# Two sets of DRAM weight sums moved from behind the residual's loads into the pool stage, in a one-layer hybrid decoder kernel

## The chip, the cores and the metric

The kernel runs on one core of one Trainium2 chip. The metric is the device time of one execution in microseconds (us); of several runs the median is given. TensorE (PE in the profile) multiplies matrices, VectorE (DVE) and ScalarE (ACT) work on tiles in SBUF and PSUM, GpSimd (POOL) and SyncE (SP) are used here mostly to issue DMA transfers. Every engine works off its own queue in order.

## The reference

One decoder layer with 16 learned tokens put ahead of 512 positions of width 1024, all in float32. Cut to what matters here:

```python
u = rmsnorm(h, mix_norm_w[i])
proj = u @ w_in[i]                        # pool, z, xbc, dt and gate columns
gates = jax.nn.sigmoid(proj[..., OFF_GATE:] + b_gate[i])
y_pool = pool_mixer(u_pool, pool_w_group[i], pool_scale[i]) @ w_pool_up[i]
y_ssd = mamba2_branch(z, xbc, dt_raw, ...) @ w_ssd_out[i]
h = h + (gate_pool * y_pool + gate_ssd * y_ssd) @ w_o[i]
v = rmsnorm(h, mlp_norm_w[i])
hid = jax.nn.relu(v @ w_ff1[i])           # 1024 -> 4096
h = h + (hid * hid) @ w_ff2[i]            # 4096 -> 1024
out = rmsnorm(h, final_norm_w)            # the 16 tokens are dropped
```

`pool_mixer` takes, for four groups of 256 channels, the mean over the last 2, 4, 8 or 16 positions less the value itself, and multiplies each group by a 256x256 matrix.

## The kernel before

Every float32 product is made of three products in a rounded format: each operand is split into a high part (a cast on ScalarE, tiles `whi`, `shi`) and the residue (a subtraction on VectorE, `wlo`, `slo`), and TensorE multiplies high by high, high by low and low by high. So each weight block of 128x1024 (512 KB) that SyncE loads (`raw`) costs a cast, a subtraction and its matmuls. `raw` tiles come from a pool of three, and SyncE waits for one to be free before it issues the next load.

Large products are done by a scheme with seven instead of eight partial products (Winograd's form of Strassen's). It needs sums of weight quarters, called t1, t2, s3 and t4. These are not formed on an engine: GpSimd issues DMA transfers from DRAM to DRAM, plain copies and accumulating ones, that build the sums in DRAM tiles (`wsum`; `f_t`, `f_s` in the profile). One such group is a set. There are 15 sets, in a fixed order: two for the scan's weights (`fx`), six for `w_ff1` (`f1`), seven for `w_ff2` (`f2`). A set of `fx` or `f1` is 8 transfers of 512 KB, four of them accumulating; a set of `f2` is 4, two of them accumulating. An accumulating transfer waits on GpSimd's queue until the copy that it adds to has landed, and blocks the queue while it waits.

The stages, in order of time in the profile:

- 0 to about 470 us: norm, projections and the scan of eight groups. The first 11 sets are issued here, spread out by a list `SETS_AT` and tied to small copies on GpSimd (L800).
- about 470 to 553 us: the pool stage. GpSimd loads back the accumulator (`acc`, L1056) and the gates (`m1`, L1090; `m<-gate_d` in the profile). `pool_pair` (L976 on) is called four times: it loads two weight blocks (L126), forms sums of their halves on VectorE (`sm`, and the first block overwritten; L985 to L990), splits them (`split_form`, L132 and L133: whiA, whiS, whiD, whiB and wloA to wloB) and makes seven products on TensorE (L1004, L1007), of which VectorE makes the moving averages (`pw`, `pu`). `pool_mix` multiplies by the group matrix (`pg`), `gate_ssd` makes the second gate (`pgs`).
- about 553 to 629 us: the merge (`pup` and the remaining `pgs`).
- about 629 to 671 us: the product with `w_o` (`wo_...`), added to the residual tile `ht`, which GpSimd loads at L1202 as soon as its SBUF, held by `u` until the last gate's matmul, comes free. Behind these four loads GpSimd issues what is left of the sets.
- about 671 us to the end: the MLP. `ff1_plain` (`pf`), `ff1_pair` (`px`) and `prod` (`alpha`, `p`, `q`: the products with `w_ff2`), which `onto` (L1240) adds to `ht` on VectorE.

The program is written in one order; a planner then orders each engine's queue by that order, by what is ready, and by edges. `with tc.issue_after(x)` gives an edge to `x` to those instructions of the block that are on the same engine as `x`, and to no others. The lines that the change touches, and the transfers of a set:

```python
def weight_steps():
    t = sets.pop(0)
    ...
    yield put(o["t1"], src[B11])                          # L777
    yield put(o["s3"], src[B12])                          # L778
    yield put(o["t1"], src[B12], accum_op=ALU.add)        # L779
    if "t2" in o:
        yield put(o["t2"], src[B22])                      # L781
    yield put(o["s3"], src[B22], accum_op=ALU.add)        # L782
    if "t2" in o:
        yield put(o["t2"], o["t1"], accum_op=ALU.add)     # L784
        yield put(o["t4"], src[B21])                      # L785
        yield put(o["t4"], o["t2"], accum_op=ALU.add)     # L786
```

```python
for t in range(4):
    ht_load = nc.gpsimd.dma_start(ht[:, t, :], x[t * P : (t + 1) * P, :])   # L1202
while sets:
    with tc.issue_after(ht_load.ins):
        ht_load = weight_sums()
```

`weight_sums()` issues one whole set and returns its last transfer. `SETS_POOL` is 0 before, so that four sets are left for the loop behind the `ht` loads: f1 number 4, f2 number 5, f1 number 5, f2 number 6, in that order, 24 transfers. The sets numbered f1 4 and f2 5 are read in the last part of the MLP.

## Time and profile before

| | us |
|---|---|
| median of 3 runs (999.92 to 1001.16) | 1000.0 |
| the profiled execution's own time | 1001.71 |
| its span, first to last instruction | 1000.0 |
| TensorE busy | 987.8 |
| VectorE busy | 803.9 |
| ScalarE busy | 602.2 |
| GpSimd busy | 119.5 |

In the rows of the profile, `out<-in` names the tiles an instruction writes and reads, L is the line of the kernel, x the number of instructions, and the brackets say how long the engine stood idle before it and what ended that. In the timeline a row begins with start and duration in us. In the rows of DMA issues the last number is the median time from issue to landing. SPq and POOLq mark the queue that issued a transfer.

### The profile page before, as it was taken

The numbers are of one execution on the slowest core, as the hardware profiler recorded it, in microseconds if no ns is written. First come the engines' busy times: TensorE is split into PE (matmuls) and PEld (weight loads), VectorE is DVE, ScalarE is ACT, GpSimd is POOL, SyncE is SP. The second block draws the span as 40 slices with busy tenths as digits, with TensorE's granted clock in tenths as the row PEclk, the third lists the DMA queues.
The fourth block names the chain that finished last, engine by engine and source line by source line (L and its number), as shares of the span: only waits on it lengthen the run. The fifth ranks groups of instructions, "written<-read, shape, count | busy, mean of one in ns | idle before, by whom it ended". The sixth has DMA issues, their size and how long they took to land.

```text
span 1000.0 us, 15672 instructions
## 1 busy us (share of the span) xinstructions
PE 987.8 (99%) x6035; PEld 873.8 (87%) x6035; DVE 803.9 (80%) x1162; ACT 602.2 (60%) x855; POOL 119.5 (12%) x215
## 2 busy tenths in 40 slices
PE   9999999999999999999999999999999999999997
PEld 7889998989889999978898888888789999999986
DVE  7978997879845888988789666975988888888885
ACT  7657839495924658574345433477666656656654
POOL 0011321211212212223200001121000000000000
PEclk9999999999999999999999999999999999999999
DMA  7284968666798848768723723899354454454332
GB/s 261 78 254 149 268 197 214 190 191 212 230 271 235 245 129 259 226 163 171 271 85 127 253 85 112 228 243 314 92 190 148 148 190 144 152 186 150 129 106 85
DMA packets 61803, 184.52 MB, mean 185 GB/s; under 512 B 7072, under 2 KB 8416, under 8 KB 60704
## 3 DMA queue, kind: packets, MB, share of 16 engines
q1 hardware_dynamic: 39456, 109.00, 32.7%
q0 software_dynamic: 18240, 67.51, 26.4%
q10 hardware_dynamic: 4032, 7.00, 1.9%
q8 instruction: 47, 0.77, 0.3%
q14 instruction: 28, 0.23, 0.1%
HBM read 173.13 MB, written 58.59 MB: 232 GB/s over the span
## 4 chain that ended last, share of the span: by engine, by line
PE 93%; ACT 3%; DVE 2%; DMA 1%; issue 0%; SPq 0%; ACTq 0%; DVEq 0%
PE px L1465 8%; PE px L215 8%; PE alpha L1533 6%; PE pz L215 6%; PE px L1468 4%; PE px L218 4%; PE alpha L1536 3%; PE pgp L215 3%; PE pz L218 3%; PE pgs L215 3%; PE py L694 2%; PE pqx L509 2%; PE pso L146 1%; PE pgp L218 1%; PE wo_alpha L1226 1%; PE po L688 1%
## 5 line engine op out<-in xcount | busy, mean ns | idle before, releaser
L113 DVE TENSOR_TENSOR wlo<-raw,whi 128x1024 fp32r<-128x1024 f32 (+2 forms) x88 | 102.0, 1171 | 46.8 <-ACT whi L111 31.0
L111 ACT CAST whi<-raw 128x1024 fp32r<-128x1024 f32 (+2 forms) x88 | 87.2, 1011 | 70.3 <-PE pso L147 15.3
L215 PE MATMUL px<-uh,whi 128*128 128x264 f32 (+1 forms) x320 | 80.9, 291 | 0.0
L218 PE MATMUL px<-ul,whi 128*128 128x264 f32 (+1 forms) x320 | 78.8, 285 | 0.0
L1240 DVE TENSOR_TENSOR ht<-ht,alpha 128x1024 f32<-128x1024 f32 x35 | 42.7, 1220 | 29.1 <-PE alpha L1533 29.1
L215 PEld LDWEIGHTS px<-uh,whi 128*128 128x128 f32 x320 | 60.4, 189 | 0.9 <-issue 0.7
L1162 ACT CAST shi<-rawf 128x1024 fp32r<-128x1024 f32 x42 | 44.2, 1053 | 28.0 <-PE alpha L1536 18.3
L218 PEld LDWEIGHTS px<-ul,whi 128*128 128x128 f32 x320 | 60.2, 188 | 0.4 <-issue 0.2
L1533 PE MATMUL alpha<-shi,hh 128*128 128x512 f32 x140 | 55.3, 395 | 2.0 <-DVE ht L1240 1.9
L1536 PE MATMUL alpha<-shi,hl 128*128 128x512 f32 x140 | 54.7, 391 | 0.0
L1163 DVE TENSOR_TENSOR slo<-rawf,shi 128x1024 fp32r<-128x1024 f32 x42 | 51.2, 1219 | 0.6 <-ACT shi L1162 0.6
L1468 PE MATMUL px<-vsl,shi 128*128 128x256 f32 x192 | 47.4, 280 | 0.0
L1465 PE MATMUL px<-vsh,shi 128*128 128x256 f32 x192 | 47.4, 281 | 0.0
L215 PE MATMUL pz<-uh,whi 128*128 128x512 f32 x112 | 43.7, 390 | 0.0
L218 PE MATMUL pz<-ul,whi 128*128 128x512 f32 x112 | 43.6, 389 | 0.0
L215 PE MATMUL px<-uh,wlo 128*128 128x264 f32 (+1 forms) x320 | 41.8, 283 | 0.0
L215 PEld LDWEIGHTS px<-uh,wlo 128*128 128x128 f32 x320 | 39.9, 188 | 0.0
L1533 PE MATMUL alpha<-slo,hh 128*128 128x512 f32 x140 | 37.4, 389 | 0.0
L1465 PEld LDWEIGHTS px<-vsh,shi 128*128 128x128 f32 x192 | 36.2, 188 | 0.9
L1468 PEld LDWEIGHTS px<-vsl,shi 128*128 128x128 f32 x192 | 36.1, 188 | 0.9
L1468 PE MATMUL px<-vl,shi 128*128 128x256 f32 x144 | 36.1, 283 | 0.0
L1465 PE MATMUL px<-vh,shi 128*128 128x256 f32 x144 | 36.0, 282 | 0.0
(599 smaller groups left out, 3064.8 us busy)
## 6 DMA issues: line engine op xcount, KB each, us to landing
raw<-in_w SPq DMA_DIRECT2D x96, 512.0 KB, 4.4
f_t<-in_f POOLq DMA_DIRECT2D x38, 512.0 KB, 7.4
f_s<-in_f POOLq DMA_DIRECT2D x26, 512.0 KB, 7.3
b<-in_f SPq DMA_DIRECT2D x21, 512.0 KB, 4.5
rawf<-in_f SPq DMA_DIRECT2D x36, 256.0 KB, 2.9
rawf<-f_t SPq DMA_DIRECT2D x36, 256.0 KB, 2.9
abc<-acs_d POOLq DMA_DIRECT2D x8, 1024.0 KB, 7.6
f_t<-f_t POOLq DMA_DIRECT2D x12, 512.0 KB, 6.7
```

The lines of the kernel that those rows point to most:

```text
L111: act.copy(hi[:, c], raw[:, c])
L113: dve.tensor_tensor(lo[:, c], raw[:, c], hi[:, c].bitcast(F32), op=ALU.subtract)
L215: pe.matmul(o, wt, rhs[0][k][:, c], start=part == 0 and k == 0, stop=part == 1 and k == NK - 1)
L218: mm[0] = pe.matmul(o, wt, rhs[1][k][:, c], start=False, stop=False)
L509: at = pe.matmul(o, wk, f[k][0], start=start and not low and k == 0, stop=stop and low == 1 and k == 3, skip_group_check=True)
L1162: splits.append((act.copy(hi, src), dve.tensor_tensor(lo, src, hi.bitcast(F32), op=ALU.subtract)))
L1163: dve.tensor_tensor(lo, src, hi.bitcast(F32), op=ALU.subtract)))
L1240: added[0] = dve.tensor_tensor(o, o, src, op=op)
L1465: pe.matmul(ps, m, f[k][0], start=start and not low and k == 0, stop=stop and low == 1 and k == 3, skip_group_check=True)
L1468: pe.matmul(ps, m, f[k][1], start=False, stop=False, skip_group_check=True)
L1533: pe.matmul(ps[t], hh[:, p, seg, st], m, start=bool(first and not low and p == 0), stop=bool(last and low and p == 1), skip_group_check=True)
L1536: pe.matmul(ps[t], hl[:, p, seg, st], m, start=False, stop=False, skip_group_check=True)
```

## The change

The first two of the four remaining sets (f1 number 4 and f2 number 5, 12 transfers) are issued behind the last load of a gate in the pool stage, at the turn n = 1 of its loop, by an edge on GpSimd's queue. The unused loop at the head of the stage is taken out. The two sets that are left stay behind the `ht` loads.

```diff
-SETS_POOL = 0
+SETS_POOL = 2
...
     for d in range(NK):
         t_load = nc.gpsimd.dma_start(acc[d], acc_d[d])
-    for _ in range(SETS_POOL):
-        with tc.issue_after(t_load.ins):
-            t_load = weight_sums()
     pend = [pooled_halves(*a) for a in pool_pair(POOL_ORDER[0])]
...
             for d in MERGE:
                 with tc.issue_after(mixed[0].ins):
                     if d < NK - 1:
-                        nc.gpsimd.dma_start(m1[d], gate_d[d])
+                        t_load = nc.gpsimd.dma_start(m1[d], gate_d[d])
+            for _ in range(SETS_POOL):
+                with tc.issue_after(t_load.ins):
+                    t_load = weight_sums()
```

## The prediction

> **What bounds the kernel now.** I read the page first, then the table of stretches, then the waits of TensorE, then the order of time around its one late wait.

> ```profile
> PE 987.8 (99%) x6035; PEld 873.8 (87%) x6035; DVE 803.9 (80%) x1162; ACT 602.2 (60%) x855; POOL 119.5 (12%) x215
> ```

> TensorE (PE) is busy for 987.8 of 1000.0 us. Whatever the change does to the queues, it can only give back what TensorE idles behind the place that it touches, or open a new idle time there. So the question is where TensorE idles from 488 us on, the earliest time at which a moved transfer can start.

> ```profile
> core 0: us, PE busy (x) PEld busy (x) DVE busy (x) ACT busy (x) POOL busy (x), PEclk, DMA share, GB/s
> 488.00:525.00 37.00, 37.00 (x243) 34.12 (x242) 33.67 (x50) 15.84 (x24) 0.16 (x1) 1.00 0.33 118
> 619.00:665.00 46.00, 46.00 (x211) 37.98 (x211) 38.00 (x46) 22.91 (x37) 11.81 (x19) 1.00 0.84 240
> 665.00:692.00 27.00, 27.00 (x127) 22.30 (x127) 16.46 (x31) 20.98 (x40) 4.91 (x7) 1.00 1.01 301
> 720.00:740.00 20.00, 18.00 (x102) 15.41 (x101) 18.67 (x24) 11.52 (x16) 0.00 (x0) 1.00 0.51 160
> ```

> Each row is a stretch: TensorE's busy time comes second, the granted clock (1.00 throughout) and the share of the 16 DMA engines stand near the end. TensorE is full in the first three and lacks 2.00 us in the last. The transfers, on the other hand, are at 0.33 in the pool stage and at their limit (1.01) from 665 to 692 us. The waits of TensorE, and then its timeline and VectorE's (DVE), say what the 2 us are:

> ```profile
> PE alpha L1533 <- DVE ht L1240: 1.9, 1, 1.9
> ```

> ```profile
> 719.70 1.07 PE L1533 MATMUL alpha<-slo,hh 128*128 128x512 f32 x4
> ...
> 725.37 0.47 PE L1533 MATMUL alpha<-shi,hh 128*128 128x512 f32 x1 [1.89 <-DVE ht L1240]
> ```

> ```profile
> 724.01 1.22 DVE L1240 TENSOR_TENSOR ht<-ht,alpha 128x1024 f32<-128x1024 f32 x1
> ```

> One product of the second MLP matrix ends at 720.77 us. The next one into the same bank must wait until VectorE has added the first to `ht`. VectorE could have begun at 720.8 and begins at 724.01, because its queue is behind. Where it fell behind is seen some 35 us earlier, on ScalarE (ACT) and on VectorE:

> ```profile
> 681.03 1.18 ACT L1571 ACTIVATE ht<-ht,m 128x1024 f32<-128x1024 f32 x1
> 686.24 1.05 ACT L111 CAST whi<-raw 128x1024 fp32r<-128x1024 f32 x1 [4.04 <-DMA raw<-in_w]
> ```

> ```profile
> 687.33 1.23 DVE L113 TENSOR_TENSOR wlo<-raw,whi 128x1024 fp32r<-128x1024 f32 x1 [5.40 <-ACT whi L111]
> ```

> ScalarE is free at 682.2 and stands 4.04 us for a weight block; VectorE stands 5.40 us behind it. The DMA issues of two stretches give that block's landing time (issued at 673.15), and that of six others of the same size issued between 577 and 620 us:

> ```profile
> raw<-in_w SPq DMA_DIRECT2D x1, 512.0 KB, 13.0
> ```

> ```profile
> raw<-in_w SPq DMA_DIRECT2D x6, 512.0 KB, 3.4
> ```

> 13.0 us instead of 3.4. GpSimd's (POOL's) queue shows whose transfers are in the way:

> ```profile
> 486.41 1.75 POOL L1090 DMA_DIRECT2D m<-gate_d  x3 [0.37 <-DMA raw<-in_w]
> 619.06 1.58 POOL L1202 DMA_DIRECT2D ht<-in_x  x3 [130.90 <-PE pgs L215]
> 620.85 0.53 POOL L1202 DMA_DIRECT2D ht<-in_x  x1 [0.21 <-issue]
> 621.37 0.53 POOL L777 DMA_DIRECT2D f_t<-in_f  x1
> ...
> 656.21 0.82 POOL L782 DMA_DIRECT2D f_s<-in_f  x1 [0.43 <-DMA f_s<-in_f]
> 656.75 0.83 POOL L777 DMA_DIRECT2D f_t<-in_f  x1
> ```

> After the last gate load (488.2 us) the queue stands 130.90 us for the residual's tile, then issues four weight-sum sets one after another. The first two, twelve transfers, are all issued from 621.37 to 656.21; the third starts at 656.75 and, with the fourth, fills the stretch in which the block was late.

> **The change part by part.** It adds no transfer and no arithmetic: 12 transfers of 512 KB (8 for the set of `w_ff1`, 4 for that of `w_ff2`) move from behind the four `ht` loads to right behind the last gate load. That edge holds on GpSimd's own queue; the `with` on `mixed[0]`, a ScalarE instruction, holds nothing there, as the gate loads leave by 488 us, long before that mix. So the moved sets start at about 488.2.

> What leaves the tail: the two sets that stay now take the place of the first two. Their form is the same (8 and then 4 transfers), so by the rows above they are issued from about 621.4 to 656.2, and the last two land some 8 us later, about 664 (my estimate from the landing of the last addition, issued at 656.21). The four `ht` loads stay where they are and meet the same company. From 665 on SyncE's (SP's) loads have the DMA engines to themselves. Of the 13.0 us only the neighbours on SyncE's own queue are left; even three blocks of 3.4 us one after another would be 10.2 us, so the block would be there by 683.4, and by overlap probably by 677; ScalarE needs it at 682.2. I take the wait of 4.04 us as gone. VectorE then starts its backlog about 4 us sooner. It needs 3.25 us (724.01 less 720.77) to meet the product on time. So TensorE's 1.89 us go, and with them the remaining 0.11 of the 2.00, a gap at 730.0 behind the next addition to `ht`. The first matmul after a wait takes 0.47 us, which I count as 0.1 more. Sum here: minus 2.1 us. It can't be more, since TensorE has no other wait behind 488 us worth naming; it is nothing if VectorE is late for another reason.

> What the pool stage gets: twelve transfers beside the loads of its weights. By the old spacing from first issue to last landing (621.4 to 664, 42.7 us) they end at 531 at the latest; with fewer loads ahead of them I expect about 525. GpSimd waits between them for its own earlier transfers; queued behind are only the `ht` loads, which can't go before 619.06, so that wait has 88 us of cover. Their bytes are read back only in the second half of the MLP. What is exposed is SyncE's loads between 488 and 531. Two have little cover. The first is the second weight block of the third pair, in SyncE's queue, its landing time, and the VectorE rows that follow it:

> ```profile
> 507.19 0.33 SPq L126 DMA_DIRECT2D raw<-in_w  x1
> ```

> ```profile
> raw<-in_w SPq DMA_DIRECT2D x1, 512.0 KB, 3.4
> ```

> ```profile
> 511.76 0.69 DVE L985 TENSOR_TENSOR sm<-raw,raw 128x512 f32<-128x512 f32 x1
> ...
> 519.14 1.22 DVE L133 TENSOR_TENSOR wloD<-raw,whiD 128x1024 fp32r<-128x1024 f32 x1
> ```

> ```profile
> 520.65 0.65 PE L1004 MATMUL pxx<-t0h,wloD 128*128 128x264 f32 x4
> ```

> It lands at 510.6 and is first read at 511.76: 1.2 us free. From there VectorE runs without a pause to the residue `wloD`, ready at 520.36, and TensorE uses that at 520.65: 0.3 us free. So a load that takes longer than 4.9 us (3.4 + 1.2 + 0.3) stops TensorE by the excess. The second is the first block of the fourth pair, issued at 520.39:

> ```profile
> 524.00 1.06 ACT L132 CAST whiA<-raw 128x1024 fp32r<-128x1024 f32 x1 [3.25 <-DVE pu L1026]
> ```

> ```profile
> 528.66 0.68 DVE L974 TENSOR_TENSOR pl<-pu,ph 128x512 fp32r<-128x512 f32 x1
> ```

> ```profile
> 530.17 0.39 PE L147 MATMUL pg<-pl,whi 128*128 128x512 f32 x1
> ```

> Its cast follows 3.6 us after the issue, so at once on landing; both queues run in order, and the `pl` that TensorE reads at 530.17 is ready at 529.34. There 0.8 us are free, and a load of over 4.4 us costs the excess.

> No row shows these loads beside such sums, so I bound them by loads that were. Here are, from two earlier stretches, a load issued at 409.88 beside one accumulating transfer (issued at 409.80), and one issued at 154.04 beside an accumulation (153.99), a plain copy and a store:

> ```profile
> f_t<-in_f POOLq DMA_DIRECT2D x1, 512.0 KB, 6.2
> raw<-in_w SPq DMA_DIRECT2D x1, 512.0 KB, 3.6
> ```

> ```profile
> raw<-in_w SPq DMA_DIRECT2D x1, 512.0 KB, 9.6
> ```

> By the first both places cost nothing. By the second the first place costs 4.7 us and the second 5.2, less what the first already gave it in time. At 507 us I expect the dependent accumulation of the set alone in flight (it stood 18 us behind the start in the old order), at 520 the last two additions. That is nearest to the 3.6 us, and I take 0; a gain is excluded, as TensorE has no idle time there (37.00 of 37.00).

> [...]

> The sum: the profiled execution took 1001.71 us, its span 1000.0 and 1.7 around it; it becomes 999.6, span 997.9. The median of the runs shown is 1000.0, 1.7 below that execution, and less 2.1 it is **997.9 us**.

> **The rivals.** *The pool stage eats part of it.* One or both tight loads take 5 to 7 us: 0.3 to 2.1 us lost, time 998.2 to 1000.0. For it: landing times near the sums vary from 3.6 to 9.6. Against it: the pool stage's DMA engines are at 0.33.

> *Slower: the weight block of the third pair comes late.* If the end of the first set and the two copies that open the second coincide with the load at 507.19, as at 154.04, it takes 9.6 us, VectorE stops at `sm`, and TensorE stops at the residue for 4.7 us: 1000.0 - 2.1 + 4.7 = 1002.6; with the second place late too, up to 1005. It decides from a load of 7.0 us on (4.9 + 2.1). For it: VectorE is busy for 33.67 of 37 us there, so that nothing is caught up, and the set's transfers come in bursts. Against it: by the spacing in the old order the burst falls 6 to 8 us behind that load's issue or, if the set runs faster, just beside the landing.

> *The stall stays.* VectorE may be late for its own amount of work: it is busy for 18.67 of 20 us at the stall. Then nothing is gained: 1000.0. Against it: it had 5.40 us of idle time on one row in the same backlog.

> *The order changes.* The order on the queues is a planner's; moved transfers may let it put VectorE's or ScalarE's instructions another way. One 128x1024 subtraction (1.22 us) ahead of a residue that has 0.3 us free costs 0.9; a few would undo the gain and more: 999 to 1003. Nothing in the profile speaks for it.

> **How the numbers follow.** 0.2%, 2.0 us, is about what a measurement of this kernel can tell from no change. The forecast, 0.50, lies 2.1 us below, just over that line: 0.38 over it and 0.12 short of it. Part eaten: 0.14, within. Slower by the late block: 0.24, of which 0.22 beyond 2 us and 0.02 within. Stall stays: 0.06, within. Order: 0.06, 0.04 slower and 0.02 within. Together faster 0.38, same 0.36, slower 0.26. The range begins at 997.2, since the runs shown spread by 1.2 us and the gain has a ceiling; above it takes in the first late load at its bound (1002.6) and leaves out both late: 1002.8. The likeliest case alone is 997.2 to 998.6.

> **What would show it.** Right: f-set transfers on GpSimd from 488 to about 525; the block of 673 us landing in under 9; no wait of `whi` near 686 and none of `alpha` on `ht` near 725; TensorE full from 490 to 550. Wrong: a wait of TensorE on `wloD`, `whiS` or `pl` in the pool stage, with `sm` idle on a DMA before it; or the `alpha` wait still there although the block landed early; or a different order on VectorE.

## The result and the profile after

| | before | after |
|---|---|---|
| median, us (4 runs each, one chip) | 1000.58 | 1007.38 |
| lowest to highest, us | 999.92 to 1001.93 | 1005.47 to 1008.22 |
| the profiled execution, us | 1001.71 | 1007.03 |

The ratio is 1.0065 (95% interval 1.0053 to 1.0077): the change costs 6.8 us, where 997.9 us was forecast and 1002.8 was the upper end. The order of instructions on TensorE, VectorE, ScalarE and SyncE is the same in both kernels; only GpSimd's queue differs, by the twelve transfers. In the changed kernel the gate loads are L1087 instead of L1090.

The tail looks as forecast. The table of stretches of the changed kernel (columns as before):

```profile
526.00:530.00 4.00, 4.00 (x20) 3.29 (x19) 0.33 (x1) 0.58 (x1) 0.00 (x0) 1.00 0.97 324
530.00:534.00 4.00, 2.02 (x7) 0.82 (x5) 3.49 (x5) 2.38 (x5) 0.00 (x0) 1.00 0.23 95
534.00:538.00 4.00, 3.20 (x8) 2.56 (x9) 4.00 (x8) 1.50 (x2) 0.00 (x0) 0.51 0.00 0
538.00:542.00 4.00, 4.00 (x22) 3.82 (x21) 2.90 (x4) 1.47 (x4) 0.00 (x0) 0.64 0.00 0
...
665.00:692.00 27.00, 27.00 (x134) 22.43 (x133) 21.29 (x38) 23.80 (x49) 0.00 (x0) 1.00 0.60 186
720.00:740.00 20.00, 20.00 (x102) 16.95 (x101) 18.59 (x28) 12.90 (x18) 0.00 (x0) 1.00 0.46 145
```

From 665 to 692 the DMA engines are at 0.60 instead of 1.01, and from 720 to 740 TensorE lacks nothing. The loss is in the first four rows: TensorE is busy for 2.02 of 4 us from 530 on, and in the two stretches of 4 us behind that its granted clock is 0.51 and 0.64 on average. Its waits, and its own timeline there:

```profile
PE pg L147 <- DVE pl L974: 2.3, 2, 1.2
...
PE pg L146 <- ACT ph L973: 0.5, 1, 0.5
```

```profile
527.91 0.39 PE L215 MATMUL pgs<-uh,whi 128*128 128x512 f32 x1
528.14 0.39 PE L218 MATMUL pgs<-ul,whi 128*128 128x512 f32 x1
...
531.32 0.50 PE L146 MATMUL pg<-ph,whi 128*128 128x512 f32 x1 [0.52 <-ACT ph L973]
532.99 0.50 PE L147 MATMUL pg<-pl,whi 128*128 128x512 f32 x1 [1.17 <-DVE pl L974]
533.33 0.39 PE L146 MATMUL pg<-ph,whi 128*128 128x512 f32 x1
534.80 0.80 PE L147 MATMUL pg<-pl,whi 128*128 128x512 f32 x1 [1.09 <-DVE pl L974]
...
536.25 0.63 PE L146 MATMUL pg<-ph,whi 128*128 128x512 f32 x1
536.67 0.63 PE L147 MATMUL pg<-pl,whi 128*128 128x512 f32 x1
```

Three waits, 2.78 us in all. Behind the third, matmuls of the same size start 0.42 us apart (536.25 to 536.67), where it was 0.23 ahead of the first (527.91 to 528.14). What TensorE waits for is on ScalarE's and VectorE's timelines:

```profile
529.42 1.05 ACT L132 CAST whiA<-raw 128x1024 fp32r<-128x1024 f32 x1 [7.54 <-DMA raw<-in_w]
530.38 0.37 ACT L1030 COPY pu<-pxx 128x264 f32<-128x264 f32 x1
530.65 1.14 ACT L973 CAST ph<-pu 128x512 fp32r<-128x512 f32 x2
```

```profile
530.51 1.22 DVE L133 TENSOR_TENSOR wloA<-raw,whiA 128x1024 fp32r<-128x1024 f32 x1 [4.18 <-ACT whiA L132]
531.65 0.69 DVE L962 TENSOR_TENSOR pw<-pw 128x513 f32<-128x513 f32 x1
532.25 0.69 DVE L974 TENSOR_TENSOR pl<-pu,ph 128x512 fp32r<-128x512 f32 x1
...
534.06 0.68 DVE L974 TENSOR_TENSOR pl<-pu,ph 128x512 fp32r<-128x512 f32 x1
```

`ph` and `pl` need nothing of the fourth pair's block, but they stand behind its cast and its residue in two in-order queues. ScalarE stands 7.54 us for the block. This is the second place of the prediction. The landing times in the changed kernel: the load issued at 521.52 (the second place), that of 508.33 (the first place), that of 680.71 (the block of the tail), and the two additions of the second set, issued at 519.00 and 520.25:

```profile
raw<-in_w SPq DMA_DIRECT2D x1, 512.0 KB, 7.8
...
raw<-in_w SPq DMA_DIRECT2D x1, 512.0 KB, 4.3
...
raw<-in_w SPq DMA_DIRECT2D x1, 512.0 KB, 4.6
...
f_t<-in_f POOLq DMA_DIRECT2D x1, 512.0 KB, 5.3
...
f_s<-in_f POOLq DMA_DIRECT2D x1, 512.0 KB, 8.8
```

The tail's block takes 4.6 us instead of 13.0, and the first place's 4.3 is under its 4.9. The second place's load took 3.5 us before and takes 7.8 beside the two additions.

All these kernels make TensorE's matmuls in one order (but for a dozen between 543 and 563 us in the two kernels that load a block again), so the start of each can be compared with that of the same matmul in the first profile of before. The rows are the kernels of the next section. The table gives how much later a kernel is at 488 us of that profile, and by how much that lag grows in each stretch behind it. 488 us is before the change can act; what stands in the column "by 488" is the difference of two executions.

| lag, us | by 488 | 488 to 528 | 528 to 530.3 | 530.3 to 560 | 560 to 719 | 719 to 726 | end |
|---|---|---|---|---|---|---|---|
| after | +1.12 | +0.02 | +3.49 | +2.93 | 0 | -2.14 | +5.31 |
| after, again | +2.21 | -0.02 | +4.37 | +1.72 | -0.04 | -2.14 | +5.99 |
| one set moved | +0.57 | -0.02 | 0 | 0 | -0.02 | -2.13 | -1.73 |
| sets in the merge | +2.23 | -0.02 | 0 | 0 | +1.20 | -2.13 | +1.14 |
| halves first | +2.17 | +0.50 | +0.01 | +0.79 | -0.05 | -2.13 | +1.15 |
| load doubled | -0.41 | +0.16 | +4.08 | +2.69 | 0 | -0.39 | +6.17 |
| half load doubled | +0.96 | -0.02 | +3.35 | +1.45 | 0 | -1.17 | +4.61 |
| additions plain | +1.25 | +0.21 | +0.85 | +0.41 | -0.01 | -2.14 | +0.43 |
| split | +0.76 | +1.34 | 0 | 0 | 0 | -2.13 | -0.14 |
| three sets early | +0.70 | -0.03 | +0.01 | -0.01 | -0.02 | -2.13 | -1.62 |
| six copies | +1.53 | -0.02 | 0 | 0 | -0.02 | -2.13 | -0.75 |

"528 to 530.3" holds the stop and the slow restart, "530.3 to 560" the halved clock.

### The profile page after: what moved, and what is told of

It reads as the page before. It is cut to its first block, busy times and chain, and to the rows that moved or that the text cites. A ratio compares the mean times of both kernels' runs of the same rounds, so it can differ in the third digit from the quotient of the medians.

```text
span 1005.3 us, 15673 instructions
## 1 busy us (share of the span) xinstructions
PE 992.2 (99%) x6035; PEld 877.0 (87%) x6035; DVE 804.3 (80%) x1162; ACT 602.1 (60%) x855; POOL 120.6 (12%) x215
## 4 chain that ended last, share of the span: by engine, by line
PE 92%; ACT 3%; DMA 2%; DVE 2%; issue 0%; SPq 0%; ACTq 0%; DVEq 0%
PE px L1465 8%; PE px L215 8%; PE alpha L1533 6%; PE pz L215 6%; PE px L1468 4%; PE px L218 4%; PE alpha L1536 3%; PE pgp L215 3%; PE pz L218 3%; PE pgs L215 3%; DMA raw<-in_w 2%; PE py L694 2%; PE pqx L509 2%; PE po L688 2%; PE pso L146 1%; PE pgp L218 1%
## 5 line engine op out<-in xcount | busy, mean ns | idle before, releaser
L113 DVE TENSOR_TENSOR wlo<-raw,whi 128x1024 fp32r<-128x1024 f32 (+2 forms) x88 | 101.9, 1171 | 42.2 <-ACT whi L111 24.5
L111 ACT CAST whi<-raw 128x1024 fp32r<-128x1024 f32 (+2 forms) x88 | 87.2, 1010 | 67.6 <-PE pso L147 15.3
L215 PE MATMUL px<-uh,whi 128*128 128x264 f32 (+1 forms) x320 | 80.9, 291 | 0.0
L1240 DVE TENSOR_TENSOR ht<-ht,alpha 128x1024 f32<-128x1024 f32 x35 | 42.7, 1219 | 29.2 <-PE alpha L1533 29.2
L215 PEld LDWEIGHTS px<-uh,whi 128*128 128x128 f32 x320 | 60.5, 189 | 0.9 <-issue 0.7
L1533 PE MATMUL alpha<-shi,hh 128*128 128x512 f32 x140 | 55.2, 395 | 0.0
L215 PE MATMUL pz<-uh,whi 128*128 128x512 f32 x112 | 43.7, 391 | 0.0
L215 PE MATMUL px<-uh,wlo 128*128 128x264 f32 (+1 forms) x320 | 41.8, 283 | 0.0
L215 PEld LDWEIGHTS px<-uh,wlo 128*128 128x128 f32 x320 | 39.9, 189 | 0.0
L1533 PE MATMUL alpha<-slo,hh 128*128 128x512 f32 x140 | 37.4, 390 | 0.0
## 6 DMA issues: line engine op xcount, KB each, us to landing
raw<-in_w SPq DMA_DIRECT2D x96, 512.0 KB, 4.6
f_t<-in_f POOLq DMA_DIRECT2D x38, 512.0 KB, 6.8
f_s<-in_f POOLq DMA_DIRECT2D x26, 512.0 KB, 6.7
b<-in_f SPq DMA_DIRECT2D x21, 512.0 KB, 4.6
f_t<-f_t POOLq DMA_DIRECT2D x12, 512.0 KB, 6.5
```

The costliest lines, as they stand in the source:

```text
L111: act.copy(hi[:, c], raw[:, c])
L113: dve.tensor_tensor(lo[:, c], raw[:, c], hi[:, c].bitcast(F32), op=ALU.subtract)
L215: pe.matmul(o, wt, rhs[0][k][:, c], start=part == 0 and k == 0, stop=part == 1 and k == NK - 1)
L1240: added[0] = dve.tensor_tensor(o, o, src, op=op)
L1533: pe.matmul(ps[t], hh[:, p, seg, st], m, start=bool(first and not low and p == 0), stop=bool(last and low and p == 1), skip_group_check=True)
```

## The experiments

**Is it the second set's additions?** The first of the two sets alone is moved.

```diff
-SETS_POOL = 2
+SETS_POOL = 1
```

> Only the first of the two sets (f1 number 4, eight transfers) is moved into the pool stage; f2 number 5 stays behind the residual's loads, with the two others. Theory A (the loss comes from the second set's two additions, which meet the weight load of about 521 us; TensorE stops 2.8 us and its clock is then halved for 6 us): the moved set is issued by about 515 us and has landed by about 520, so that load takes 3.4 to 4.4 us as before, TensorE does not wait for pl near 531 and keeps a clock of 1.00 there. Behind the residual there are 16 transfers instead of 12, issued from 621 to about 668, so most of the 1.9 us wait at 725 is still saved: 998 to 1000.5 us. Rival B (any weight sums in the pool stage cost the time, whichever transfers they are): a wait of 1 to 3 us in the pool stage and a halved clock remain, 1002 to 1006 us.

Measured 1000.16 us beside 1000.99 of the kernel before on the same chip (0.9994, 0.9986 to 1.0003). The load at 520.94 and a stretch:

```profile
raw<-in_w SPq DMA_DIRECT2D x1, 512.0 KB, 3.6
```

```profile
530.00:534.00 4.00, 4.00 (x24) 3.49 (x24) 4.00 (x7) 3.02 (x4) 0.00 (x0) 1.00 0.00 0
```

TensorE is full, its clock 1.00. The time is within theory A's figures; rival B's wait and lower clock aren't there: the eight transfers of the first set in the pool stage cost nothing in this profile.

**Does the load cost only by the order of the queues?** All transfers stay; the casts and subtractions of the pooled halves (`halved_by` holds the second pair's last ones) go ahead of the block's.

```diff
-        fa = split_form(a1, both, f"A{p}")
-        behind = behind or (None, None)
+        with after(*(halved_by if p == POOL_ORDER[3] else ())):   # the last ph, pl
+            fa = split_form(a1, both, f"A{p}")
+        behind = behind or ((halved_by[1], None) if p == POOL_ORDER[3] else (None, None))
```

> The changed kernel with all its transfers where they are; two edges put the cast and the subtraction of the fourth pair's first block (whiA, wloA), and the sum sm, behind the casts ph and the subtractions pl of the second pair on ScalarE's and VectorE's queues. Theory A (the load is late, but it costs only because ph and pl stand behind its cast in two in-order queues): the load of 521 us still takes 6 to 9 us, but ph and pl are done by about 526 and TensorE does not wait at 531; at most 1 us is lost where wloA or wloS is first used; clock 1.00: 998 to 1000.5 us. Rival C (the transfers slow TensorE directly, or the lower clock comes from something other than its waiting): clock again near 0.5 to 0.6 for some us behind 534, 1003 to 1007 us.

Measured 1000.76 (1.0002, 0.9992 to 1.0011). The landing of the block (issued at 523.20) and ScalarE's timeline:

```profile
raw<-in_w SPq DMA_DIRECT2D x1, 512.0 KB, 7.6
```

```profile
527.49 1.14 ACT L975 CAST ph<-pu 128x512 fp32r<-128x512 f32 x2 [0.19 <-DVE pu L964]
530.83 1.05 ACT L132 CAST whiA<-raw 128x1024 fp32r<-128x1024 f32 x1 [2.20 <-DMA raw<-in_w]
```

The load is as late as in the changed kernel (7.6), yet TensorE doesn't stop near 531 and its clock stays at 1.00 there: `ph` is cast before the block lands. The median is 0.3 us above theory A's figures and far below rival C's. These edges give back nearly all of the 6.8 us of the change, with every transfer where it was. What is lost there is 0.50 and 0.79 us (table). The 0.50 is the first place: the load of 509.34 took 5.2 us, over its 4.9. The 0.79 is lost from 538 to 541, at the products that use the fourth pair's `whiD`.

**Does the wait halve the clock, or do the transfers?** No set is moved. The fourth pair's first block is loaded twice, one more 512 KB load on SyncE's queue, with edges that keep the queues near their order; in essence:

```diff
+        for _ in range(again):          # 1, for the fourth pair's first block
+            nc.sync.dma_start(a1, w[block])
```

> The kernel before, with no sets moved, and with the first weight block of the fourth pair loaded twice into the same tile (one more 512 KB load on SyncE's queue, which waits for the first to land); edges keep the order of ScalarE, VectorE and TensorE there near to that of before, ph and pl behind whiA and wloA. Theory A (a stop of TensorE of 2 to 3 us in all near 531 us halves its clock for some 6 us, whatever made it stop): the block is there 3.3 to 4 us later than before, TensorE waits 2.3 to 3 us, and its clock falls to about 0.5 for 4 to 7 us: 1004 to 1007 us. Rival C (the halved clock comes from GpSimd's transfers or from the DMA engines at their limit): only the wait, clock 1.00: 1002.5 to 1003.7 us.

Measured 1007.50 beside 1000.99 (1.0059, 1.0047 to 1.0072), 0.5 us above theory A's figures.

```profile
530.90 0.49 PE L148 MATMUL pg<-ph,whi 128*128 128x512 f32 x1 [1.50 <-ACT ph L980]
532.99 0.80 PE L148 MATMUL pg<-pl,whi 128*128 128x512 f32 x1 [1.59 <-DVE pl L982]
```

```profile
530.00:534.00 4.00, 1.51 (x3) 1.01 (x4) 4.00 (x6) 1.96 (x4) 0.00 (x0) 0.77 0.00 0
534.00:538.00 4.00, 4.00 (x11) 3.16 (x10) 3.96 (x6) 2.67 (x3) 0.00 (x0) 0.50 0.00 0
```

With no transfer of GpSimd near, and the DMA engines at 0.00 in both stretches, TensorE waits 3.09 us and its clock is 0.50 behind. Rival C falls: the clock is halved behind the stop without those transfers. The same with half of the block:

> As the kernel with the doubled load (nothing of the sets moved), but only half of the fourth pair's first block is loaded a second time, a smaller dose of the same delay. By theory A the block is complete 2 to 3 us later than before and TensorE waits 1 to 2.2 us in all near 531. Whether its clock is then halved tells where the point lies between the 1.9 us after which it stayed at 1.00 at 725 us and the 3.1 us after which it fell: if it falls, 1002.5 to 1005 us; if not, 1001.5 to 1003 us.

Measured 1005.65 (1.0051, 1.0032 to 1.0069).

```profile
531.36 0.50 PE L148 MATMUL pg<-ph,whi 128*128 128x512 f32 x1 [0.77 <-ACT ph L980]
533.45 0.79 PE L148 MATMUL pg<-pl,whi 128*128 128x512 f32 x1 [1.59 <-DVE pl L982]
```

```profile
534.00:538.00 4.00, 4.00 (x15) 3.19 (x14) 3.96 (x6) 2.89 (x4) 0.00 (x0) 0.66 0.00 0
```

It was not a much smaller dose: 2.36 us of waits where 1 to 2.2 were expected, and the clock falls here too (1.45 us lost), so that the time is 0.65 us above the figures for that.

**Is it that they accumulate?** The second set's two additions become plain copies.

```diff
-        yield put(o["t1"], src[B12], accum_op=ALU.add)
+        yield put(o["t1"], src[B12], **({} if t == ("f2", 5) else {"accum_op": ALU.add}))
```

(and the same for `s3`; the sums of this set are left out)

> The changed kernel with the second set's two additions turned into plain copies of the same pieces (the sums of that set are left out): the same number of transfers at the same places, none of them accumulating beside the load of 521 us. [...] Theory G (any two GpSimd transfers there do it): the load takes over 6.5 us, waits of 2 us or more and the halved clock stay, ratio 1.004 to 1.007.

Measured 1002.95 beside 1001.00 (1.0019, 1.0010 to 1.0028). The load at 521.97, TensorE's wait, and the stretch behind it:

```profile
raw<-in_w SPq DMA_DIRECT2D x1, 512.0 KB, 5.0
```

```profile
PE pg L147 <- DVE pl L975: 0.7, 1, 0.7
```

```profile
534.00:538.00 4.00, 4.00 (x32) 3.88 (x31) 4.00 (x7) 2.07 (x4) 0.00 (x0) 1.00 0.00 0
```

The load takes 5.0 us, one short wait of 0.7 us is left and the clock stays at 1.00: the load of over 6.5 us and the ratio of 1.004 to 1.007, which theory G had for any two transfers of GpSimd, aren't there. Of the 4.3 us that the load was late in the first profile of the changed kernel, the accumulating form made 2.8. The two copies landed sooner than the additions, too (4.1 and 5.4 us against 5.3 and 8.8). The prediction's row of 3.6 us also had an addition beside the load, but a single one, issued 0.08 us ahead of it; here there are two, issued 2.5 and 1.3 us ahead. Which of these two differences counts was not tried.

**Elsewhere.** Both sets in the merge:

```diff
+        if n == 3:                      # loop of the merge
+            t_load = pool.tensor_copy(seen, acc[d][:, :1])
+            for _ in range(SETS_POOL):
+                with tc.issue_after(t_load.ins):
+                    t_load = weight_sums()
```

> Both sets are taken out of the pool stage and issued in the merge instead, tied to a small GpSimd copy at about 575 to 581 us, so that all twelve transfers are issued before the residual's loads at 619. Theory A: the pool stage is that of the kernel before (load of 521 us in 3.5 us, no wait for pl, clock 1.00), the wait at 725 us is gone as in the changed kernel, and the merge's weight loads have cover: 998 us, 997.5 to 999. Rival B (twelve transfers between loads stop TensorE wherever they are put): a new wait of TensorE on wlo or whi between 580 and 615 us, 1000 to 1005 us.

Measured 1002.03 (1.0010, 1.0001 to 1.0018): theory A missed, and though the time is within rival B's figures, its wait between 580 and 615 us isn't there. The copy came at 596.29, not at 580, so the sets were still running when the residual's turn came. GpSimd's queue and TensorE's waits:

```profile
624.55 0.82 POOL L782 DMA_DIRECT2D f_s<-in_f  x1 [0.47 <-DMA f_s<-in_f]
625.09 2.46 POOL L1204 DMA_DIRECT2D ht<-in_x  x4
```

```profile
PE wo_q L1231 <- DVE l_m L1105: 1.1, 1, 1.1
```

The `ht` loads leave at 625.09 instead of 619.06, VectorE waits 1.16 us for them, and TensorE behind it. The two remaining trials put the second set, or the second and a third, at n = 0 of that loop, with the first in the pool stage:

> The first of the two sets (f1 number 4) in the pool stage as in the changed kernel, the second (f2 number 5, four transfers) in the merge, tied to a small GpSimd copy behind the first gated sum at about 560 us; the two last sets stay behind the residual's loads. Theory A: the four transfers run from 560 to about 577 us beside merge loads that have cover, the load of 521 us takes 3.5 us, no wait and no lower clock near 531, and the wait at 725 us is gone: 998.0 to 999.5 us on a chip where the kernel before takes 1000.6 to 1001, that is 0.9975 to 0.9990 of it. Rival D (the gain of the tail is less in most executions than the 1.9 us of the profiled one): 0.9990 to 1.0000.

> As the last, with a third set (f1 number 5, eight more transfers) put into the merge as well, from about 577 to 605 us, so that only f2 number 6 is left behind the residual's loads. Theory A: the tail from 640 to 692 us is now almost free of weight sums, no new wait elsewhere: like the split kernel or up to 0.5 us better, 0.9970 to 0.9990 of the kernel before. Rival B (weight sums stop TensorE wherever weight loads have to be shared): a wait of 1 us or more between 580 and 640 us, 1.0000 or above.

Measured 1001.04 (1.0001, 0.9989 to 1.0014) and 1000.57 (1.0000, 0.9987 to 1.0014), beside 1000.78. No stop and no lower clock near 531, the wait at 725 gone, no new wait between 580 and 640, and still no gain: this speaks for rival D. In the first of them the load of the first place (507.93) took this:

```profile
raw<-in_w SPq DMA_DIRECT2D x1, 512.0 KB, 6.0
```

and the lag grew by 1.34 us from 488 to 528. The pool stage is the same as with one set moved and with three sets early, where this load took 4.2 and 4.7 us and the lag grew by nothing: whether the first place is late differs from execution to execution.

**Where is the gain?** The changed kernel and the kernel before once more, for further profiles.

> The changed kernel once more, for the spread of its executions beside those of the kernel before on the same chip. Theory A: again waits for ph and pl near 531 us of 2 to 3.5 us in all and a halved clock behind them of 4 to 7 us; 1.005 to 1.008 of the kernel before. Rival E (the waits and the lower clock of the first profile were an accident of one execution): the waits are under 1 us in this profile, ratio under 1.003.

> The kernel before once more, for a second profile. Theory A: the wait for ht at 725 us is 1.9 us again, so that the tail's gain is worth as much in most executions. Rival D (that wait varies): it is under 1.2 us here.

The changed kernel again: 1007.50 beside 1000.78 (1.0059, 1.0038 to 1.0079), with the second place's load at 8.7 us. So that is no accident of one execution. But the wait of the kernel before at 725 us is. Its second profile has no row for `alpha` at all among the waits. Four more profiles of it followed.

> The kernel before, a third profile, to see in how many of its executions TensorE waits near 725 us. Theory H (the block issued at about 673 lands at a time that the queue of sums sets, about 686; TensorE reaches 725 earlier or later by what it has lost before, so that the wait is 1.9 us where it has lost least and nothing where it comes 1.5 us later): if TensorE starts the matmuls of 719.70 in the first profile within 0.3 us of that time, the wait is 1.5 to 2.1 us; if it starts them over 1 us later, the wait is under 0.7 us.

> The kernel before, a fourth profile, with the same expectation as the third: the sum of what TensorE lost ahead of 719 us (against the first profile) and its wait near 725 us is 1.5 to 2.3 us by theory H; by rival D, that the wait comes and goes with the DMA engines alone, the two are unrelated.

> The kernel before, a fifth profile, for the count of executions with the wait near 725 us. Theory I: under 0.7 us. Rival: 1.5 to 2.1 us.

> The kernel before, a sixth profile, as the fifth. Theory I: under 0.7 us. Rival: 1.5 to 2.1 us.

| profile of before | 1st | 2nd | 3rd | 4th | 5th | 6th |
|---|---|---|---|---|---|---|
| lag at 719 us against the 1st | 0 | +1.54 | +1.05 | +2.61 | +0.22 | +3.18 |
| lag gained from 719 to 726 | 0 | -1.79 | -1.72 | -1.78 | -1.94 | -2.13 |
| wait for `ht` near 725 | 1.9 | none | 0.2 | none | none | none |

The wait of 1.9 us is in one of six, and one of 0.2 us in another. In the fifth, TensorE came as early as in the first, but the block (issued at 673.37) was there sooner; its landing, ScalarE's wait for it, and the stretch:

```profile
raw<-in_w SPq DMA_DIRECT2D x1, 512.0 KB, 11.1
```

```profile
684.55 1.05 ACT L111 CAST whi<-raw 128x1024 fp32r<-128x1024 f32 x1 [1.06 <-DMA raw<-in_w]
```

```profile
720.00:740.00 20.00, 19.86 (x116) 17.20 (x115) 18.09 (x22) 12.34 (x17) 0.00 (x0) 1.00 0.59 181
```

11.1 us instead of 13.0 is enough. So theory H, by which TensorE's own lateness sets the wait, doesn't hold in general. It fits the third profile; in the fourth there is no wait, as by H, but the lag of 2.61 is already above the sum of 1.5 to 2.3 that H gave; it doesn't fit the fifth. The kernel with the doubled load, whose tail is that of before, speaks against it too: TensorE comes 6.5 us later there, the same block is issued at 679.67 and takes 12.6 us, and the wait is 1.5 us. Taking the two sets from the tail gains 0 to 0.4 us there in five profiles of six (the difference of the lags from -2.13), and not 2.1. The upper bound was tried too: six plain copies in place of the two sets, whose additions are left out.

```diff
+        if t in (("f1", 4), ("f2", 5)):
+            for n, q in zip(o, (B11, B12, B22, B21)):
+                yield put(o[n], src[q])
+            return
```

> The changed kernel with the two moved sets replaced by six plain copies (the additions of these two sets are left out), issued at once from 489 us. Nothing waits for a transfer of their own, the copies have landed by about 502 us, and the tail is that of the changed kernel. So this is the most that taking the two sets from the tail can give. Theory I (the 1.9 us wait of the first profile is there in a minority of the executions of the kernel before): ratio 0.9990 to 1.0005. Rival (it is there in most, and something in the pool stage or the merge ate the gain of the other kernels): 0.9970 to 0.9985.

Measured 999.98 beside 1001.96 (0.9984, 0.9974 to 0.9994), which is outside theory I's figures and inside the rival's. What speaks for theory I is the count of the profiles, not this time. On this chip 9 of 17 runs of the kernel before had a mean granted clock of 0.998 or less, and one of the 12 of this kernel. In five of the seven profiles with such a mean and no lower clock behind 531, the clock is halved for a while near 446 us, ahead of anything that differs; in the other two it is lower only at the end of the span. Among the runs with a mean of 0.999 or more the medians are 999.74 (11 runs) and 1000.53 (8 runs), 0.8 us apart. How much of the 0.16% is the emptied tail, these runs don't settle.

## Why the prediction was wrong, point by point

- **What bounds the kernel**: right. All that moved the time is where TensorE stops, or runs at a lower clock behind a stop, and the order on its queue did not change (the rival of the planner's order falls).
- **The gain of 2.1 us**: the mechanism was read rightly and was seen to vanish (block in 4.6 us, TensorE full from 720 to 740), but its size was one execution's. The step that failed is the sum: it took a wait from an execution of 1001.71 us and subtracted it from a median of 1000.0, of executions of which, going by the six profiles, most have no such wait. The prediction named the 1.7 us between the two and did not ask whether the wait was part of it. In size: 2.1 forecast, 0 to 0.4 in five of six profiles. The kernels with fewer sets in the tail and no stop in the pool stage (one set moved, three sets early, six copies) measure 0.9994, 1.0000 and 0.9984 of the kernel before.
- **The first place**: threshold about right. By the prediction a load that takes longer than 4.9 us "stops TensorE by the excess": loads of 4.3, 5.2 and 6.0 us cost 0.02, 0.50 and 1.34, which is some 0.2 us more than the excess. Its price of 0 was right in both profiles of the changed kernel, in part by luck: with the same transfers it was 0.50 in the kernel of the halves.
- **The second place**: threshold right, value wrong, and this is the step that decided. The excess over 4.4 is 3.4 us for 7.8 and 4.3 for 8.7; the lags are 3.49 and 4.37. I put two additions beside that load and took the row of 3.6 us, a load beside one addition, as the nearest. The row of 9.6 us, with an addition and two more transfers, came nearer to what was measured. The timing was called right ("the last two additions" at 520); the price was not.
- **The slower rival**: right in kind, wrong in its place. It put the late block at the third pair; it was the fourth pair's. Even its 1005 us for both places late, which the range left out, is 2.4 us under what was measured.
- **What had no price at all**: the clock, which the sum left at 1.00 behind a stop. A stop of 2.4 to 3.7 us cost 1.4 to 2.9 us more. With this the medians close: 3.5 to 4.4 for the stop, 1.7 to 2.9 for the clock, next to nothing from the tail, 6.1 to 6.4 together, against 6.8 and 6.7 measured.

## What to carry to other kernels

Before a wait of one profile is priced as a gain, take a second profile of the unchanged kernel: the wait of 1.9 us was in one of six here. Price a moved transfer by what it runs beside and by its form (7.8 us for the load beside two additions, 5.0 beside two copies), put the excess over the cover on the bill, and add a second item for the clock: behind stops of 2.4 to 3.7 us near 531 it cost 1.4 to 2.9 us more here (the section below has the rows). Where a late load stops work that doesn't need it, try a few edges in the order of the queues: here they were worth nearly as much as moving the transfers back (1000.76 us beside 1000.99 of the kernel before).

## What was not expected of the hardware

TensorE's clock. These stops and the clock behind them were seen (us waited, lowest granted clock in stretches of 4 or 5 us):

| where | waited | clock behind |
|---|---|---|
| additions plain, 531 | 0.7 | 1.00 |
| merge, 637 | 1.1 | 1.00 |
| 441 to 444, all 17 profiles | 1.4 to 1.5 | 1.00 in 10, lower in 7 |
| load doubled, 731 | 1.5 | 1.00 |
| first profile of before, 725 | 1.9 | 1.00 |
| half load doubled, 531 | 2.36 in two | 0.66 |
| after, 531 | 2.78 in three | 0.51 |
| load doubled, 531 | 3.09 in two | 0.50 |
| after again, 531 | 3.7 in three | 0.65 |

The row of 441 to 444 as the stretch of 444 to 449 shows it, in the first profile of before and in its fourth, the same instructions behind the same wait:

```profile
444.00:449.00 5.00, 4.93 (x35) 3.92 (x36) 5.00 (x7) 2.72 (x5) 1.80 (x2) 1.00 0.72 100
```

```profile
444.00:449.00 5.00, 4.31 (x24) 3.38 (x25) 5.00 (x9) 3.01 (x5) 1.80 (x2) 0.72 0.60 66
```

Such an episode is worth some 1.6 us (the lag of the first profile of the changed kernel grows by 1.58 from 440 to 449 us), and it is a part of the spread between executions of one kernel.

```profile
530.67:534.08 3.41, 1.35 (x4) 0.48 (x3) 3.41 (x6) 1.71 (x4) 0.00 (x0) 1.00 0.08 32
534.08:537.49 3.41, 2.69 (x6) 2.18 (x7) 3.41 (x7) 0.99 (x2) 0.00 (x0) 0.50 0.00 0
537.50:540.91 3.41, 3.41 (x14) 3.10 (x13) 3.19 (x5) 1.43 (x2) 0.00 (x0) 0.50 0.00 0
540.91:544.32 3.41, 3.41 (x30) 3.41 (x29) 1.57 (x4) 1.85 (x3) 0.00 (x0) 1.00 0.00 0
...
530.60:534.01 3.41, 1.74 (x7) 0.89 (x5) 1.57 (x2) 2.65 (x5) 0.00 (x0) 1.00 0.52 213
534.01:537.42 3.41, 1.41 (x5) 0.89 (x6) 3.41 (x7) 0.30 (x1) 0.00 (x0) 1.00 0.00 0
537.42:540.84 3.42, 3.42 (x11) 2.76 (x10) 3.42 (x6) 2.14 (x3) 0.00 (x0) 0.50 0.00 0
```

In these profiles near 531 the busy time of TensorE within one step goes with the clock, and the length of the stop does not. Behind steps with 1.35 and 1.41 us the clock is halved, and so it is with the doubled load (1.15) and with half of it (1.20); behind 1.74 us it is not, nor near 725 us in the first profile of before (1.89). The full clock came back behind steps in which TensorE was busy for 3.41 and 3.42 us; behind 2.69 us, and 2.58 with the doubled load, it stayed halved for another step. So the second profile's longer stop, which is spread over two steps, had the shorter episode. Counted from the 7.05 and 5.01 us at which the two records begin, the steps lie differently about the same instructions. The waits of 441 to 444 don't fit the border that these rows would set: in the first profile of the changed kernel the clock was halved behind 1.97 us in the step, and in that of before, with 1.86, it was not. Why is open.

The other new number is what an accumulating transfer did to a neighbour, beside a copy of the same 512 KB: the load took 7.6, 7.8 and 8.7 us beside two additions in three profiles, and 5.0 us beside two copies in the one profile with them.
